# Storing one row of the first tile early, on ScalarE's queue, in an RMSNorm kernel

## The chip, the cores and the metric

The kernel runs on one core of one Trainium2 chip. The metric is the device time of one execution in microseconds (us). A span in a profile is a little shorter than that time (161.6 us against 163.42 us for the same execution of the kernel before), because it begins at the first and ends at the last profiled event. Times are compared between runs of the same chip and session, as medians. Engine names: ACT is ScalarE, DVE is VectorE, SP is the engine whose queue issues most transfers here.

## The reference, cut to what matters

```python
x: (16, 1024, 512) float32; gamma: (512,) float32
rms = np.sqrt(np.mean(x ** 2, axis=-1, keepdims=True) + 1e-5)
out = (x / rms * gamma).astype(np.float32)
```

There are 16,384 rows of 2 KB. 33.55 MB are read and 33.55 MB are written, and there is little arithmetic per byte.

## The kernel before

The rows form four tiles. A tile is 128 partitions x 32 rows of 512 numbers: 64 KB per partition, 8 MB in all, contiguous per partition both in HBM and in SBUF. The kernel keeps three tiles in SBUF ("slots"), so tile 3 goes into slot 0 again, once tile 0 has been stored. All large transfers are issued on SP's queue, in program order.

```python
def load(t, slot, r0, r1):
    nc.sync.dma_start(out=slots[slot][:, r0:r1], in_=xv[t][:, r0:r1])
def store(t, slot, r0, r1):
    nc.sync.dma_start(out=ov[t][:, r0:r1], in_=slots[slot][:, r0:r1])

load(0, 0, 0, 16)
load(0, 0, 16, 32)
load(1, 1, 0, 32)
load(2, 2, 0, 32)
# ... gamma is broadcast to all partitions ...
def compute(slot, r0, r1):
    for g in range(r0, r1, G):      # G = 8 rows
        # ACT: 8 x Square with a sum per row, then one Sqrt
        # DVE: one reciprocal, then 8 x (row * rstd * gamma), in place
        # ...

compute(0, 0, 32)
store(0, 0, 0, 32)
compute(1, 0, 16)
store(1, 1, 0, 16)
load(3, 0, 0, 16)                   # waits until slot 0 is stored
load(3, 0, 16, 32)
compute(1, 16, 32)
store(1, 1, 16, 32)
compute(2, 0, 32)
store(2, 2, 0, 32)
compute(0, 0, 16)                   # tile 3
store(3, 0, 0, 16)
compute(0, 16, 32)
store(3, 0, 16, 32)
```

Of the kernel before, what the change touches and what calls it, by code (L numbers as in the profile page):

```python
# [1 line left out]

# [4 lines left out]


@with_exitstack
def kernel(  # L10
    ctx: ExitStack,
    tc: tile.TileContext,
    x: bass.AP,
    gamma: bass.AP,
    out: bass.AP,
):
    nc = tc.nc
    P = nc.NUM_PARTITIONS
    eps = 1e-5
    fp32 = mybir.dt.float32  # L20
    AF = mybir.ActivationFunctionType
    OP = mybir.AluOpType

    xf = x.flatten_outer_dims()
    of = out.flatten_outer_dims()
    N, D = xf.shape
    R = 32
    G = 8
    assert N == 4 * P * R

    xv = xf.rearrange("(t p r) d -> t p r d", p=P, r=R)
    ov = of.rearrange("(t p r) d -> t p r d", p=P, r=R)

    const = ctx.enter_context(tc.tile_pool(name="const", bufs=1))
    stats = ctx.enter_context(tc.tile_pool(name="stats", bufs=4))
    psum = ctx.enter_context(tc.tile_pool(name="psum", bufs=1, space=bass.MemoryType.PSUM))

    slots = [const.tile([P, R, D], fp32, name=f"slot{i}") for i in range(3)]
# [12 lines that stand above are left out]
    gamma_row = const.tile([1, D], fp32)  # L51
    nc.scalar.dma_start(out=gamma_row, in_=gamma.unsqueeze(0))
    ones_col = const.tile([1, P], fp32)
    nc.vector.memset(ones_col, 1.0)  # L54
    gamma_psum = psum.tile([P, D], fp32)
    nc.tensor.matmul(gamma_psum, ones_col, gamma_row, start=True, stop=True)  # L56
    gamma_b = const.tile([P, D], fp32)
    nc.vector.tensor_copy(out=gamma_b, in_=gamma_psum)  # L58

    eps_t = const.tile([P, 1], fp32)  # L60
    nc.vector.memset(eps_t, eps)  # L61
    sq_scratch = const.tile([P, D], fp32)

    def compute(slot, r0, r1):
        for g in range(r0, r1, G):
            ss = stats.tile([P, G], fp32, name="ss")
            rms = stats.tile([P, G], fp32, name="rms")
            rstd = stats.tile([P, G], fp32, name="rstd")
            for r in range(G):
                nc.scalar.activation(  # L70
                    out=sq_scratch,
                    in_=slots[slot][:, g + r, :],
                    func=AF.Square,
                    accum_out=ss[:, r : r + 1],
                )
            nc.scalar.activation(out=rms, in_=ss, func=AF.Sqrt, bias=eps_t, scale=1.0 / D)  # L76
            nc.vector.reciprocal(out=rstd, in_=rms)  # L77
            for r in range(G):
                nc.vector.scalar_tensor_tensor(  # L79
                    out=slots[slot][:, g + r, :],  # L80
                    in0=slots[slot][:, g + r, :],
                    scalar=rstd[:, r : r + 1],
                    in1=gamma_b,
                    op0=OP.mult,
                    op1=OP.mult,
                )

    compute(0, 0, 32)
    store(0, 0, 0, 32)
    compute(1, 0, 16)  # L90
    store(1, 1, 0, 16)
    load(3, 0, 0, 16)
# [5 lines that stand above are left out]
    compute(0, 0, 16)  # L98
# [5 lines that stand above are left out]
# [1 line left out]
_INS = ['x', 'gamma']  # L105
_OUTS = [((16, 1024, 512), 'float32')]


# [23 lines left out]
```

## Time and profile before

| | kernel before |
|---|---|
| time, three runs | 163.3 us median (163.19 to 163.88) |
| span of the profiled run | 161.6 us |
| ACT busy, DVE busy | 98.5 us (61%), 90.4 us (56%) |
| moved by DMA | 67.14 MB, 415 GB/s over the span |

These are lines of the page of the kernel before: the busy time of each engine, the share of the 16 DMA engines that was busy in each of 40 equal slices (in tenths), the DMA packets, and the queue of SP (q1).

```profile
span 161.6 us, 509 instructions
PE 2.0 (1%) x2; PEld 0.5 (0%) x2; DVE 90.4 (56%) x147; ACT 98.5 (61%) x274; POOL 0.2 (0%) x4
...
DMA  7999999989989999699699999999999799699991
...
DMA packets 1733, 67.14 MB, mean 415 GB/s; under 512 B 193, under 2 KB 193, under 8 KB 194
...
q1 hardware_dynamic: 1728, 67.11, 97.3%
```

ACT and DVE are idle for more than a third of the span. The DMA engines are busy throughout (the digits below 9 come from counting, as explained below). What counts is therefore how long each packet keeps its DMA engine. The packet records of the trace give that (they are read from the trace itself; no view of the profile prints them): a packet of 64 KB (one partition's part of a tile) takes 2.418 us, one of 32 KB takes 1.213 us, and on each engine one follows the other with no gap of note (the eight packets of tile 1 per engine took 19.37 us on the median engine, 2.421 us each). No 64 KB packet of this trace is shorter than 2.418 us. 16 engines x 65,536 B / 2.418 us is 434 GB/s, which is called line rate below.

The windows view makes packets visible that take longer. Here are four windows of the kernel before. The last two columns are the busy share of the DMA engines and the GB/s that they moved. Whole packets are counted at their start, so both can exceed what is possible (1.19 and 516 in the second line), but they do so together.

```profile
core 0: us, PE busy (x) PEld busy (x) DVE busy (x) ACT busy (x) POOL busy (x), PEclk, DMA share, GB/s
26.00:36.00 10.00, 0.00 (x0) 0.00 (x0) 8.72 (x16) 9.59 (x29) 0.00 (x0) 1.00 0.97 420
36.00:44.00 8.00, 0.00 (x0) 0.00 (x0) 7.36 (x12) 4.66 (x14) 0.00 (x0) 1.00 1.19 516
44.00:56.00 12.00, 0.00 (x0) 0.00 (x0) 7.46 (x14) 11.52 (x33) 0.00 (x0) 1.00 1.00 432
56.00:68.00 12.00, 0.00 (x0) 0.00 (x0) 10.72 (x18) 11.50 (x35) 0.00 (x0) 1.00 0.94 360
```

At line rate, 420 GB/s needs a share of 420 / 434 = 0.97, which is what the first line has. In the last window 360 GB/s need 0.83, but the share is 0.94: (0.94 - 360/433.6) x 12 us = 1.32 us per engine went by without bytes. This number is called the **stall** below. (From the rounding of the share it is good to about 0.06 us.) The packets show where it is: all 16 engines lengthen exactly one packet, the last load packet of tile 2, just before the first big store, from 2.418 to between 3.3 and 3.97 us.

The chain of waits of the kernel before shows what hangs on it (start, length, what):

```profile
44.85 37.78 DMA out_dram<-slot
82.64 19.40 DMA slot<-in_x_dram
```

The store of tile 0 is issued at 44.85 us, but on its queue it stands behind the load of tile 2, which lands at 63.30 us, and it has landed only at 82.6 us. Tile 3 is loaded then.

### The profile page before, as it was taken

To read this page: it belongs to the slowest core of one execution; us is meant where nothing else is said; L and a number is where in the kernel's file an instruction comes from. 1 tells how busy PE (TensorE), PEld (TensorE's weight loads), DVE (VectorE), ACT (ScalarE), POOL (GpSimd) and SP (SyncE) were. 2 spreads that over 40 slices of the span, in tenths; PEclk is the share of its full clock that TensorE was granted. 3 is DMA by queue.
4 is the path that set the end of the run, shared out by engine and by line. 5 is a ranking of instruction groups with operands and counts; after the bars stand their busy time and mean duration, and the time that the engine had idled before them with its cause. 6 is when DMAs were issued, how large, how long until landed. Compare 5 with 4: busy or idle time off the path is not lost.

```text
span 161.6 us, 509 instructions
## 1 busy us (share of the span) xinstructions
PE 2.0 (1%) x2; PEld 0.5 (0%) x2; DVE 90.4 (56%) x147; ACT 98.5 (61%) x274; POOL 0.2 (0%) x4
## 2 busy tenths in 40 slices
PE   4000000000000000000000000000000000000000
PEld 1000000000000000000000000000000000000000
DVE  0100098988909898898898892019889880000000
ACT  3007999996599999999999700799999400000000
POOL 0000000000000000000000000000000000000000
DMA  7999999989989999699699999999999799699991
GB/s 260 389 430 478 389 470 438 519 375 405 519 373 405 505 276 487 292 519 487 292 440 454 389 454 454 389 478 430 389 503 519 308 487 503 292 462 430 405 470 49
DMA packets 1733, 67.14 MB, mean 415 GB/s; under 512 B 193, under 2 KB 193, under 8 KB 194
## 3 DMA queue, kind: packets, MB, share of 16 engines
q1 hardware_dynamic: 1728, 67.11, 97.3%
q14 instruction: 3, 0.02, 0.0%
q10 hardware_dynamic: 2, 0.00, 0.0%
HBM read 33.56 MB, written 33.55 MB: 415 GB/s over the span
## 4 chain that ended last, share of the span: by engine, by line
DMA 43%; ACT 20%; DVE 17%; issue 2%; DVEq 0%
DMA out_dram<-slot 23%; DMA slot<-in_x_dram 19%; ACT sq_scratch L70 18%; DVE slot L79 16%; ACT rms L76 2%; ACT L76 1%; DVE rstd L77 1%; DVEq L127 0%
## 5 line engine op out<-in xcount | busy, mean ns | idle before, releaser
L70 ACT ACTIVATE sq_scratch<-slot 128x512 f32<-128x512 f32 x128 | 80.5, 629 | 26.8 <-DMA slot<-in_x_dram 23.2
L79 DVE SCALAR_TENSOR_TENSOR slot<-slot,rstd,gamma_b 128x512 f32<-128x512 f32 x128 | 86.2, 747 | 0.6
L77 DVE RECIPROCAL rstd<-rms 128x8 f32<-128x8 f32 x16 | 3.2, 203 | 37.7 <-ACT rms L76 37.7
L70 ACT ACTIVATION_READ_ACCUMULATOR sq_scratch<-slot 128x1 f32 x128 | 23.9, 187 | 0.0
L76 ACT ACTIVATE rms<-ss,eps_t 128x8 f32<-128x8 f32 x16 | 4.8, 301 | 0.5
L58 DVE COPY gamma_b<-gamma_psum 128x512 f32<-128x512 f32 x1 | 0.7, 692 | 3.3 <-PE gamma_psum L56 3.3
L56 PE MATMUL gamma_psum<-gamma_row,ones_col 1*128 1x512 f32 x2 | 2.0, 1119 | 2.2 <-DMA gamma_row<-in_gamma_dram 2.2
L70 ACT ACT_TABLE_LOAD x1 | 1.3, 1283 | 1.3 <-PEq L116 1.3
L76 ACT ACT_TABLE_LOAD x1 | 1.3, 1283 | 0.0
L54 DVE MEMSET ones_col<- 1x128 f32 x1 | 0.2, 165 | 0.8 <-PEq L116 0.8
L56 PEld LDWEIGHTS gamma_psum<-gamma_row,ones_col 1*128 1x128 f32 x2 | 0.5, 308 | 2.2 <-issue 2.2
L116 POOL MEMSET const-bfloat16-1.0<- 128x1 bf16 x1 | 0.1, 101 | 0.0
L116 POOL MEMSET const-uint8-127<- 128x1 uint8 x1 | 0.1, 101 | 0.0
L116 POOL MEMSET const-float32-0.0<- 128x1 f32 x1 | 0.1, 98 | 0.2 <-issue 0.2
L116 POOL MEMSET const-float32-1.0<- 128x1 f32 x1 | 0.1, 98 | 0.0
L61 DVE MEMSET eps_t<- 128x1 f32 x1 | 0.1, 59 | 0.0
## 6 DMA issues: line engine op xcount, KB each, us to landing
slot<-in_x_dram SPq DMA_DIRECT2D x4, 4096.0 KB, 19.4
out_dram<-slot SPq DMA_DIRECT2D x4, 4096.0 KB, 31.2
slot<-in_x_dram SPq DMA_DIRECT2D x2, 50.9
out_dram<-slot SPq DMA_DIRECT2D x2, 40.5
gamma_row<-in_gamma_dram ACTq DMA_DIRECT2D x1, 2.0 KB
```

The lines of the kernel that those rows point to most:

```text
L54: nc.vector.memset(ones_col, 1.0)
L56: nc.tensor.matmul(gamma_psum, ones_col, gamma_row, start=True, stop=True)
L58: nc.vector.tensor_copy(out=gamma_b, in_=gamma_psum)
L61: nc.vector.memset(eps_t, eps)
L70: nc.scalar.activation(out=sq_scratch, in_=slots[slot][:, g + r, :], func=AF.Square, accum_out=ss[:, r : r + 1],)
L76: nc.scalar.activation(out=rms, in_=ss, func=AF.Sqrt, bias=eps_t, scale=1.0 / D)
L77: nc.vector.reciprocal(out=rstd, in_=rms)
L79: nc.vector.scalar_tensor_tensor(out=slots[slot][:, g + r, :], in0=slots[slot][:, g + r, :], scalar=rstd[:, r : r + 1], in1=gamma_b, op0=O ...
L116: nc = _bacc.Bacc("TRN2", target_bir_lowering=False, num_devices=1)
```

## The change: its intent, and the diff

The intent is to begin storing earlier: one finished row of each partition (256 KB in all) leaves on ACT's queue while the loads on SP's queue still run. The bytes are the same, and only their order changes.

```diff
-    compute(0, 0, 32)
-    store(0, 0, 0, 32)
+    compute(0, 0, G)
+    nc.scalar.dma_start(out=ov[0][:, 0:1], in_=slots[0][:, 0:1])
+    compute(0, G, 32)
+    store(0, 0, 1, 32)
```

## The prediction

> **What bounds the kernel now.** The DMA engines. The page gives ACT 61% and DVE 56% of the 161.6 us span, but its DMA row is filled to the end: 67.14 MB at a mean of 415 GB/s. In the windows view a share of 1.21 goes with 524 GB/s, so 16 fully busy engines move about 433 GB/s[...]. At that rate 67.1 MB need 155 us. About 6.6 us are left: about 2 us before the first packet, about 1.3 us after the last, stragglers, and packets slower than line rate.
>
> The trace's DMA packets show those. A 64 KB packet takes 2.418 us and a 32 KB one 1.213 us nearly everywhere, back to back. Two exceptions: the first load packet of each engine (about +0.56 us), and the last load packet in front of the first store, at about 58 to 62 us, where every engine took 3.3 to 3.97 us (about +1.3 us, once). The windows view agrees: 56 to 60 us has share 1.00 with only 295 GB/s, which needs 0.68. No later store start costs over about 0.1 us. I read it as a one-time cost of the core's first store to HBM; that is not proved.
>
> **What the change does.** Bytes stay the same. 256 KB (128 packets of 2 KB, eight per DMA engine) leave the first big store, whose packets shrink from 64 to 62 KB, and go out from ACT's queue. The instruction order puts that issue on ACT after the second Square of the second group, at about 21.9 us; DVE has row 0 ready at about 21.5 us. The issue costs ACT 0.34 to 0.53 us (DMA issues in the trace), and ACT idles 3.15 us before slot 1's first Square at 42.3 us: free. The big store is issued at about 45 us either way, and its turn comes only at about 62 us: free. The small store shares the same 16 engines with the loads[...], delays them by about 0.6 us and shortens the first store by as much. If the engines switch queues after each packet, I estimate eight rounds of about 2.5 us: landing at about 42 us, far before load 3 needs slot 0 at about 82 us.
>
> Cost: a 2 KB packet took 0.116 us (gamma's), line rate is 0.076 us: about 0.3 us for eight, perhaps more for turning between loads and stores.
> Gain: if the first-store cost is paid by the small store while loads keep the engine moving, up to 1.3 us disappears. If it blocks the engine there too, it only moves to about 22 us.
> All of this is on the critical path, since every DMA microsecond is.
>
> I weigh the two about equally: gain 0.65 us, cost 0.3 us.
>
> **Prediction: 162.9 us, range 161.8 to 164.3; faster by over 2% 0.02, within 2% 0.96, slower by over 2% 0.02.**
>
> **What would show it.** Right: unchanged ACT and DVE busy times; 56 to 62 us at about 433 GB/s per full share; load 2 landing at about 62 us instead of 63.3, and the first store about 1 us before 82.6. Gain wrong: the excess appears at about 22 us and later landings don't move. Cost wrong: share without bytes between 22 and 42 us above 0.3 us.
>
> **What would make it wrong.** Small packets stalling the loads at every switch (slower by 1 us or more); 62 KB packets off line rate; the slowest engine, about 1 us behind the others now, delayed further.

## The result, and the profile after

| | before | after |
|---|---|---|
| time, six fast runs each | 163.38 us median (163.03 to 163.88) | 163.2 us median (162.72 to 163.64) |
| ratio | | 0.9986, 95% interval 0.9962 to 1.0011: the same |
| span of the profiled run | 161.6 us | 161.1 us |

A ratio is the mean time of one kernel's fast runs over that of the other's of the same rounds, so it is not quite the ratio of the medians. No difference can be told from the scatter.

The page of the changed kernel, same lines as above, and with them the row of the issued transfers that is new (size in KB, us from issue to landing):

```profile
span 161.1 us, 510 instructions
PE 2.0 (1%) x2; PEld 0.5 (0%) x2; DVE 90.4 (56%) x147; ACT 98.6 (61%) x274; POOL 0.2 (0%) x4
...
DMA  7999999969999896999799999999999799699992
...
DMA packets 1877, 67.14 MB, mean 417 GB/s; under 512 B 209, under 2 KB 209, under 8 KB 338
...
q1 hardware_dynamic: 1728, 66.85, 97.1%
q10 hardware_dynamic: 146, 0.26, 0.4%
...
out_dram<-slot ACTq DMA_DIRECT2D x1, 256.0 KB, 23.8
```

And its timeline around the issue (start, length, what):

```profile
20.74 2.08 DVE L79 SCALAR_TENSOR_TENSOR slot<-slot,rstd,gamma_b 128x512 f32<-128x512 f32 x3
...
21.11 0.63 ACT L70 ACTIVATE sq_scratch<-slot 128x512 f32<-128x512 f32 x1
21.52 0.39 ACTq L89 DMA_DIRECT2D out_dram<-slot  x1
...
21.96 0.63 ACT L70 ACTIVATE sq_scratch<-slot 128x512 f32<-128x512 f32 x1
```

The small store is issued at 21.52 us, costs ACT under 0.2 us (the next Square starts at 21.96 us, and at 21.86 us in the kernel before), and lands 23.8 us later. In the packet records each of its 2 KB packets takes 0.084 us, and most of them have a 64 KB load packet on either side: they run in rounds of 16, which begin at 26.45, 28.95, 31.44, 33.94, 36.43, 38.92 and 41.42 us, with the eighth right behind the seventh at 41.77 us. So here the two queues took turns on one set of 16 engines. The windows and the chain of the changed kernel:

```profile
26.00:36.00 10.00, 0.00 (x0) 0.00 (x0) 8.63 (x16) 9.59 (x29) 0.00 (x0) 1.00 1.00 433
36.00:44.00 8.00, 0.00 (x0) 0.00 (x0) 7.36 (x13) 4.24 (x12) 0.00 (x0) 1.00 0.95 410
44.00:56.00 12.00, 0.00 (x0) 0.00 (x0) 7.01 (x13) 11.53 (x34) 0.00 (x0) 1.00 1.01 438
56.00:68.00 12.00, 0.00 (x0) 0.00 (x0) 10.76 (x18) 11.49 (x34) 0.00 (x0) 1.00 1.07 423
```

```profile
44.94 37.45 DMA out_dram<-slot
82.46 19.45 DMA slot<-in_x_dram
```

The stall is still there: (1.07 - 423/433.6) x 12 us = 1.13 us, against 1.32 us before. And nothing was lengthened at 26 to 44 us, where the small store ran: 0.05 us in all. So the core had already written to HBM when the big store began, and the engines waited all the same. My reading of the stall was wrong, and the experiments look for what it is.

### The profile page after: what moved, and what is told of

It reads as the page before. It is cut to its first block, busy times and chain, and to the rows that moved or that the text cites. A ratio compares the mean times of both kernels' runs of the same rounds, so it can differ in the third digit from the quotient of the medians.

```text
span 161.1 us, 510 instructions
## 1 busy us (share of the span) xinstructions
PE 2.0 (1%) x2; PEld 0.5 (0%) x2; DVE 90.4 (56%) x147; ACT 98.6 (61%) x274; POOL 0.2 (0%) x4
## 4 chain that ended last, share of the span: by engine, by line
DMA 43%; ACT 20%; DVE 17%; issue 2%; DVEq 0%; ACTq 0%; SPq 0%
DMA out_dram<-slot 23%; DMA slot<-in_x_dram 20%; ACT sq_scratch L70 18%; DVE slot L79 16%; ACT rms L76 2%; ACT L76 1%; DVE rstd L77 1%; DVEq L129 0%; ACTq L89 0%; SPq L41 0%
## 6 DMA issues: line engine op xcount, KB each, us to landing
out_dram<-slot ACTq DMA_DIRECT2D x1, 256.0 KB, 23.8
```

## The experiments

The theories at the start, for the stall at 56 to 62 us:

- *issue*: it is a collision with the next store's issue at 60.5 us;
- *ring*: the first store on SP's own queue pays it;
- *size*: any 64 KB load packet followed by a store packet pays it;
- *bulk*: the first store of some length pays it, and 2 KB packets are too short.

Later ones split *bulk* into a *write side* (HBM is written for the first time, either anywhere or in each region) and a *read side* (DMA reads SBUF for the first time: until then there had been loads only, which write SBUF). In the expectations, S is the stall. The runs e, f and g were made on three chips, and a time is compared only with the kernel before on the same chip.

### Four first looks

**e1_slot1_whole**: nothing is issued at 60.5 us.

```diff
-    compute(1, 0, 16)
-    store(1, 1, 0, 16)
+    compute(1, 0, 32)
+    store(1, 1, 0, 32)
     load(3, 0, 0, 16)
     load(3, 0, 16, 32)
-    compute(1, 16, 32)
-    store(1, 1, 16, 32)
```

> Edit to the kernel before: slot 1 is stored by one 8 MB DMA after its whole compute, so that no DMA is issued near 60.5 us, where before issued the store of slot 1's first half. Stall S is the lengthening of the last load packet of each engine before the first big store (about 1.3 us per engine before, 1.14 after). Theory issue (S is a collision with the DMA issue at 60.5 us): S falls below 0.3 us and load 2 lands about 1 us earlier than 63.3. Theories ring (first store on the SP queue pays), bulk (first large store pays) and size (64 KB load packet followed by a store packet pays): S stays at 1.0 to 1.4 us.

Measured: the stall is 1.34 us, load 2 lands at 63.53 us; 163.65 us (before 163.25). *Issue* falls.

**e2_small_on_sp**: the small store of the change, on SP's queue between loads 1 and 2.

```diff
-    load(2, 2, 0, 32)      # with the other loads
     compute(0, 0, G)
-    nc.scalar.dma_start(out=ov[0][:, 0:1], in_=slots[0][:, 0:1])
+    store(0, 0, 0, 1)
+    load(2, 2, 0, 32)
```

> Edit to the changed kernel: the same 256 KB store, but issued on SP's queue between load 1 and load 2, so it runs at about 41 us as the first store of that queue. Theory ring: S at about 58 to 62 us falls below 0.3 us, and about 1 us of lengthening shows at about 39 to 43 us instead. Theory bulk: nothing over 0.3 us at 41 us, S stays 1.0 to 1.4 us at 62. Theory size: about 1 us at 41 us and again at 62 us. Theory issue: S stays at 62.

Measured: 0.38 us at 36 to 44 us, and 0.65 us at 56 to 68 us; 163.11 us (before 163.25). No theory had this. The eight 2 KB packets ran one after the other here, and on ACT's queue they ran mostly one at a time between load packets. One after the other they paid a part, and the big store paid the rest.

**e3_eight_rows**: the early store takes all eight finished rows, on ACT's queue.

```diff
-    nc.scalar.dma_start(out=ov[0][:, 0:1], in_=slots[0][:, 0:1])
+    nc.scalar.dma_start(out=ov[0][:, 0:8], in_=slots[0][:, 0:8])
     compute(0, G, 32)
-    store(0, 0, 1, 32)
+    store(0, 0, 8, 32)
```

> Edit to the changed kernel: all eight finished rows (16 KB per partition, 2 MB) go out early on ACT's queue, not one. Theory bulk: 0.5 us or more of lengthening of load packets right at the first 16 KB packets, at about 27 to 30 us, and S at 62 us below 0.5 us. Theories ring, size and issue: S stays at 1.0 to 1.4 us at about 62 us, and the early packets run within 0.05 us of line rate.

Measured: no stall at the big store (0.01 us), but 0.55 us at 26 to 36 us and 0.47 us at 36 to 44 us; 162.38 us (before 163.25). *Bulk* holds and *ring* falls, since the big store was still the first store on SP's queue. The packets show two steps: the load packet in front of the first 16 KB packet is lengthened by about 0.4 us, and the last load packet of tile 1, at about 42 us, by about 0.4 us again.

**e4_halves**: the kernel before, with 32 KB packets on both sides of the first load-to-store switch.

```diff
-    load(2, 2, 0, 32)
+    load(2, 2, 0, 16)
+    load(2, 2, 16, 32)
 ...
-    store(0, 0, 0, 32)
+    store(0, 0, 0, 16)
+    store(0, 0, 16, 32)
```

> Edit to the kernel before: load 2 and store 0 in two halves each, so the last load packet and the first store packet are 32 KB, as at the later load-to-store switch at 110 us, which cost 0.1 us. Theory size: S falls to 0.1 to 0.6 us. Theories ring, bulk and issue: S stays at 1.0 to 1.4 us.

Measured: 1.31 us; 163.97 us (before 163.25). *Size* falls.

### Which side of the store pays

All edits are to the changed kernel. In the expectations of f1 and f4 the theory *core* is a write side that is paid once, wherever HBM is written. In f1, f3 and f4 tile 0 is stored whole at its usual turn, and the 2 MB of the early transfer come on top: an estimate of 2.10 MB / 434 GB/s = 4.8 us.

**f1_other_address** (rows written to the wrong place, and overwritten later):

```diff
-    nc.scalar.dma_start(out=ov[0][:, 0:1], in_=slots[0][:, 0:1])
+    nc.scalar.dma_start(out=ov[3][:, 0:8], in_=slots[0][:, 0:8])
```

> Edit to the eight-row run: the early 2 MB go to the place of the last tile's output (they are overwritten later by the right rows), and the whole of tile 0 is stored at its usual turn. Adds 2 MB, about 4.8 us at 433 GB/s. Theory core (what is paid is a warm-up of the write path of each engine, wherever it writes): S at the first big store (now about 67 us) below 0.3 us, as in the eight-row run. Theory address (each engine pays for the output region that it first writes): S there is 0.8 us or more.

Measured: 0.65 us at 26 to 36 us, 0.23 us at 36 to 44 us, and 0.00 us at the big store; 167.17 us (before 163.03). Where in the output the early store wrote made no difference at the big store (0.00 us here, 0.01 us in e3). *Address* falls.

**f2_few_partitions**: the bytes of the change as one 16 KB packet per engine.

```diff
-    nc.scalar.dma_start(out=ov[0][:, 0:1], in_=slots[0][:, 0:1])
+    nc.scalar.dma_start(out=ov[0][0:16, 0:8], in_=slots[0][0:16, 0:8])
 ...
-    store(0, 0, 1, 32)
+    nc.sync.dma_start(out=ov[0][16:128], in_=slots[0][16:128])
+    nc.sync.dma_start(out=ov[0][0:16, 8:32], in_=slots[0][0:16, 8:32])
```

> Edit to the changed kernel: the same 256 KB go early, but as eight rows of 16 partitions: one 16 KB packet per engine in place of eight of 2 KB. Theory packet (what matters is the length of one unbroken write, and 2 KB is too short to pay anything): about 0.4 us at the early packet, at about 29 to 32 us, and S at 62 us clearly below the 1.14 us of the changed kernel, at 0.9 us or less. Theory amount (bytes written before count, whatever their cut): S at 62 us 1.0 to 1.3 us, as in the changed kernel, which wrote the same bytes. Theory address: S 1.0 to 1.3 us too, since one packet covers only an eighth of the engine's rows.

Measured: 174.43 us (before 163.03), and inconclusive for the question, because the edit brought a larger effect of its own. Its windows have 0.61 us at 26 to 36 us and 1.01 us at 56 to 68 us, so the big store kept more than the 0.9 us that *packet* allowed, as *amount* expected. But in both windows other packets than the last loads were slow too (the early 16 KB ones by 0.55 us on average), so this is no clean count of the stall. Here is its window with the store of the 16 partitions' remaining rows:

```profile
80.00:92.00 12.00, 0.00 (x0) 0.00 (x0) 10.72 (x18) 11.49 (x34) 0.00 (x0) 1.00 0.94 203
```

The engines are busy and move 203 GB/s. Of that store's sixteen 48 KB packets, eleven took 6.9 us longer on average than the 1.81 us of line rate (8.8 us in all), and the engines stayed out of step to the end. The other five ran at line rate or close to it. What slowed the eleven was not shown: no run here tests a transfer of few partitions alone.

**f3_sbuf_to_sbuf**: SBUF is read early by DMA, but HBM is not written.

```diff
-    load(2, 2, 0, 32)      # with the other loads
+    load(2, 2, 0, 24)
 ...
-    nc.scalar.dma_start(out=ov[0][:, 0:1], in_=slots[0][:, 0:1])
+    nc.scalar.dma_start(out=slots[2][:, 24:32], in_=slots[0][:, 0:8])
+    load(2, 2, 24, 32)     # loads over the copied rows
```

> Edit to the eight-row run: the early 2 MB go from slot 0 to rows 24 to 32 of slot 2 (loaded over afterwards by a load of its own), so SBUF is read early by DMA but HBM isn't written; tile 0 is stored whole at its turn. Adds 2 MB, about 4.8 us. Theory read side (S is the first read of SBUF by DMA): about 0.4 us at the first early packet, and S at the first big store below 0.3 us. Theory write side (S is the first bulk write to HBM): no stretch at the early packets, S 1.0 to 1.4 us.

**f4_hbm_to_hbm**: HBM is written early by DMA, but SBUF is not read.

```diff
-    nc.scalar.dma_start(out=ov[0][:, 0:1], in_=slots[0][:, 0:1])
+    nc.scalar.dma_start(out=ov[3][:, 0:8], in_=xv[3][:, 0:8])
```

> Edit to the eight-row run: the early 2 MB go from the input's last tile straight to the output's last tile (overwritten later), issued by ACT at the start, so HBM is written early by DMA but SBUF isn't read; tile 0 is stored whole at its turn. Adds 2 MB, about 4.8 us. Theory write side with core: S at the first big store below 0.3 us. Theory read side: S 1.0 to 1.4 us. Theory address: S 0.8 us or more.

The windows of f3_sbuf_to_sbuf:

```profile
26.00:36.00 10.00, 0.00 (x0) 0.00 (x0) 8.41 (x15) 9.31 (x28) 0.00 (x0) 1.00 1.14 473
36.00:44.00 8.00, 0.00 (x0) 0.00 (x0) 7.36 (x13) 3.25 (x10) 0.00 (x0) 1.00 0.83 328
...
56.00:68.00 12.00, 0.00 (x0) 0.00 (x0) 10.72 (x18) 11.53 (x33) 0.00 (x0) 1.00 1.05 451
```

and those of f4_hbm_to_hbm:

```profile
26.00:36.00 10.00, 0.00 (x0) 0.00 (x0) 9.32 (x15) 9.59 (x28) 0.00 (x0) 1.00 0.97 419
36.00:44.00 8.00, 0.00 (x0) 0.00 (x0) 6.75 (x12) 6.49 (x20) 0.00 (x0) 1.00 1.20 517
...
56.00:68.00 12.00, 0.00 (x0) 0.00 (x0) 10.72 (x18) 11.50 (x35) 0.00 (x0) 1.00 0.91 350
```

With the copy inside SBUF the early windows have 0.49 and 0.59 us without bytes, and the window of the first big store has 0.12 us, none of it at the switch: tile 2's last load packets (16 KB) and the first store packets run at line rate, 0.611 and 2.418 us. With the copy inside HBM the early windows have 0.04 and 0.06 us, and the big store pays 1.23 us. The times agree: 167.24 us and 168.65 us (before 163.03), which less 4.8 us are about 162.4 and 163.8 us. So **in these runs the stall belongs to the first long read of SBUF by DMA, and not to the first write to HBM.** One reservation: the copy of f4 ran from the start and had landed at 20.1 us, over 40 us before the big store's turn, while the copy of f3 landed at 53.1 us. The copy of f4 shows no bill of its own, though: in the first 20 us, by the packet records, its engines spent only 0.15 us more above line rate than those of the kernel before. And f3 by itself shows that no HBM write is needed to pay the bill. What in the read takes the time, no run shows.

### Is the bill smaller when it is paid early?

**g2_eight_rows_on_sp**: the 2 MB of the eight-row store, unbroken, on SP's queue.

```diff
-    load(2, 2, 0, 32)      # with the other loads
     compute(0, 0, G)
-    nc.scalar.dma_start(out=ov[0][:, 0:1], in_=slots[0][:, 0:1])
+    store(0, 0, 0, 8)
+    load(2, 2, 0, 32)
     compute(0, G, 32)
-    store(0, 0, 1, 32)
+    store(0, 0, 8, 32)
```

> The eight-row store on SP's queue between load 1 and load 2: the same 2 MB, now as an unbroken run of eight 16 KB packets per engine, not between load packets. Theory first bulk read of SBUF pays, whatever queue issues it: 0.9 to 1.3 us of lengthening at about 39 to 43 us, S before the big store below 0.2 us, and no gain in time over the changed kernel beyond its scatter. Rival (only the mixing with loads, or ACT's queue, removes S): S before the big store stays 0.6 us or more.

Its windows:

```profile
36.00:44.00 8.00, 0.00 (x0) 0.00 (x0) 7.36 (x13) 3.99 (x12) 0.00 (x0) 1.00 0.98 367
...
56.00:68.00 12.00, 0.00 (x0) 0.00 (x0) 10.91 (x17) 11.49 (x34) 0.00 (x0) 1.00 0.96 415
```

Measured: 1.07 us at 36 to 44 us and 0.04 us at the big store; 163.71 us, with 163.67 us before. The bill moved, all of it, and no time was won.

**g3_four_rows** (edit as in e3 with 4 for 8: 8 KB packets):

> Four rows early on ACT's queue (8 KB packets, 1 MB), between the one row of the change (S 1.14 us) and eight rows (S 0). If the payment depends on the length of a packet in steps between 2 and 16 KB: early lengthening of 0.1 to 0.4 us per engine at the first early packet and S at 62 us between 0.1 and 0.8 us. If any packet of more than a few KB pays in full: S below 0.1 us.

Measured: 0.19, 0.40 and, at the big store, 0.32 us; 162.47 us (before 163.67).

**g4_sixteen_rows** (edit as in e3 with 16 for 8, and compute(0, 0, 16) ahead of it: 32 KB packets), five rounds:

> Sixteen rows early on ACT's queue (32 KB packets, 4 MB), issued at about 33 us; candidate for a version that beats both. If the gain of eight rows comes from S being paid in parts between loads: early lengthening 0.8 to 1.1 us in all, S before the big store below 0.1 us, and a time like eight rows, ratio 0.993 to 0.998. If longer packets pay the whole at once: 1.2 us or more early, ratio 0.997 to 1.001.

Measured: 1.24 us in one step at 32 to 36 us, 0.00 us at the big store. 162.83 us median (162.5 to 163.09, six runs) against 163.67 us; ratio 0.9945, 95% interval 0.9929 to 0.9961.

**g1_eight_rows_timed**: the kernel of e3 again, five rounds.

> The eight-row kernel again, unchanged, timed against the kernel before. Its one look was 0.87 us shorter than before's. If its gain is the vanished S and a less delayed slowest engine: 0.4 to 1.1 us faster, ratio 0.993 to 0.998 with an interval below 1, and S at 62 to 67 us again below 0.1 us. If the one look was luck: ratio 0.998 to 1.002.

Measured: 162.47 us median (162.39 to 162.68, six runs) against 163.67 us (163.37 to 164.15, eleven runs); ratio 0.9927, 95% interval 0.9911 to 0.9943. This is the best version: 0.7% faster than the kernel before, clear of the scatter, though well under 2%. The changed kernel was not timed in the same session. Its own ratio to the kernel before was 0.9986, and the two intervals don't overlap. The windows of this kernel:

```profile
26.00:36.00 10.00, 0.00 (x0) 0.00 (x0) 8.52 (x16) 9.39 (x29) 0.00 (x0) 1.00 1.12 460
36.00:44.00 8.00, 0.00 (x0) 0.00 (x0) 7.36 (x13) 3.12 (x9) 0.00 (x0) 1.00 0.86 344
44.00:56.00 12.00, 0.00 (x0) 0.00 (x0) 4.50 (x9) 9.59 (x27) 0.00 (x0) 1.00 1.01 437
56.00:68.00 12.00, 0.00 (x0) 0.00 (x0) 10.72 (x19) 11.52 (x33) 0.00 (x0) 1.00 0.96 416
```

### The bill, and where 0.7% came from

All the runs but f2 side by side, computed as above; the last column is how far the last DMA engine finished behind the median engine in the last store, from the 16 completions of that store in the trace.

| run | early transfer: queue, packet | 26-36 | 36-44 | 44-56 | 56-68 us | sum | last engine behind |
|---|---|---|---|---|---|---|---|
| before | none | 0.01 | 0.00 | 0.05 | 1.32 | 1.38 | 1.58 |
| after | ACT, 2 KB | 0.01 | 0.04 | 0.00 | 1.13 | 1.18 | 1.27 |
| e1 | none | 0.01 | 0.00 | 0.05 | 1.34 | 1.40 | 1.85 |
| e2 | SP, 2 KB | 0.01 | 0.38 | 0.00 | 0.65 | 1.04 | 1.87 |
| e4 | none | 0.01 | 0.01 | 0.08 | 1.31 | 1.41 | 2.22 |
| g3 | ACT, 8 KB | 0.19 | 0.40 | -0.01 | 0.32 | 0.90 | 1.13 |
| e3 | ACT, 16 KB | 0.55 | 0.47 | 0.03 | 0.01 | 1.06 | 0.98 |
| g1 (same kernel) | ACT, 16 KB | 0.59 | 0.53 | 0.03 | 0.01 | 1.16 | 0.94 |
| f1 | ACT, 16 KB | 0.65 | 0.23 | 0.03 | 0.00 | 0.91 | 1.05 |
| f3 | ACT, 16 KB, SBUF to SBUF | 0.49 | 0.59 | 0.05 | 0.12 | 1.25 | 1.01 |
| f4 | ACT, 16 KB, HBM to HBM | 0.04 | 0.06 | 0.03 | 1.23 | 1.36 | 2.11 |
| g2 | SP, 16 KB | 0.01 | 1.07 | 0.13 | 0.04 | 1.25 | 2.09 |
| g4 | ACT, 32 KB | 1.24 | 0.01 | 0.03 | 0.00 | 1.28 | 1.17 |

The sum stays between 0.9 and 1.4 us in every run of the table: an early read of SBUF moved the bill and took about a third off it at most (1.38 to 0.90 us). In these runs, how much of it moved grew with the stretch that was read without a load packet in between. With 2 KB packets that ran mostly one by one (after) it hardly moved (1.13 us were left at the big store); with 16 KB packets between loads it moved altogether (0.01 us left in e3), and with 32 KB ones in a single step (1.24 us in g4). In g3, e3 and g4 the packets and the amount grew together, but the amount alone doesn't decide: e2 and the changed kernel read the same bytes early in the same 2 KB packets, and where eight ran in one row the big store was left with 0.65 us, otherwise with 1.13 us (the queue and the moment differed too). The second step of e3 fits: after it two 16 KB packets ran in a row, on 15 of the 16 engines. A run that holds the amount fixed and changes only the packet is missing, since f2 failed at it.

That does not yet explain why g1 (162.47 us) is faster than g2 (163.71 us, one run), which stores the same eight rows. The last column does. In these two profiled runs the median engine finished the last store at 159.05 us before and at 158.72 us in g1 (0.33 us earlier), and the last engine 1.58 us behind it before and 0.94 us in g1 (0.64 us less). Two thirds of the 0.97 us thus come from the one engine that ends last. Its lag grows in the kernel before from 1.08 us at the landing of load 3's first half to 1.56 us at that of its second half, at 112.3 us, where the queue turns from loads to stores again. In g1 it stays at 0.97 us there, and in g2 it jumps from 1.29 to 2.08 us. In all six runs with an early read of SBUF on ACT's queue in packets of 8 KB or more (e3, f1, f3, g1, g3, g4) the lag grows there by 0.11 us or less, and in the changed kernel by 0.12 us (1.12 to 1.24 us). In the others (before, e1, e2, e4, f4, g2) it grows by 0.28 us or more. That is a regularity over single profiles. Part of the lag may have a visible origin. In every page that was taken (before, after, f2, f3, f4, g1, g2) the DMA queues include q14, of kind "instruction", with three packets in the span. In the kernel before these are 8 KB each and run at 33.97, 53.25 and 82.87 us between the other packets: 0.31 us each on the engine that they hit, with the following packet lengthened by 0.31, 0.60 and 0.12 us. Followed from end to start, the packets of g1 show that the engine hit by the one at 56.8 us (0.31 us, and 0.53 us on the next packet, 0.84 us in all) is the one that ended last, with a lag of 0.94 us; in the kernel before, the same holds for the one at 53.3 us as far as the packets can be told apart. No run tests it. Why a read on ACT's queue long before spares the last engine this second delay is open.

## Why the prediction was right or wrong

- **The bound (DMA engines at line rate, about 434 GB/s): right.** ACT and DVE stayed at 98.6 and 90.4 us busy, as predicted, and the time didn't move beyond the scatter. But the changes that the prediction named as its test did not come: load 2 landed at 63.66 us (before 63.30 us, expected about 62 us), and the first store 0.23 us earlier (82.39 us) instead of about 1 us.
- **"DVE has row 0 ready at about 21.5 us", issue on ACT at about 21.9 us, free: right.** It was issued at 21.52 us and took 0.39 us; ACT's waiting for loads is 23.0 us where it was 23.2 us.
- **Landing at about 42 us: the turns were right and the time 3 us short.** It landed at 45.3 us (21.52 + 23.8). The first 2 KB packet ran only at 26.5 us, some 5 us after the issue. It harmed nothing: tile 3's load was issued at 82.46 us.
- **Cost 0.3 us for eight small packets: too high.** They took 0.084 us each where 2 KB at line rate need 0.076 us: 8 x 0.008 = 0.06 us per engine. 62 KB packets ran at line rate (2.342 us).
- **Gain 0.65 us, the mean of "disappears" and "only moves to about 22 us": this is the step that failed.** It rested on the sentence "I read it as a one-time cost of the core's first store to HBM". Neither of its two outcomes came. The small store paid nothing, and the stall stayed where it was, at 1.13 us of 1.32 us, because in these runs it is paid by the first long read of SBUF (f3 left 0.12 us at the big store, f4 1.23 us), and 2 KB packets that ran one by one between loads hardly paid it. In place of 0.65 us the stall shrank by 0.19 us, or by 0.15 us if the 16 lengthened packets themselves are averaged (from 1.28 to 1.14 us).
- **The sum held by luck, because both terms were too large.** Predicted: 0.65 - 0.3 = 0.35 us net, 162.9 us. The terms as measured, 0.19 - 0.06 (or 0.15 - 0.06), make about 0.1 us; the median engine gained 0.13 us in the last store (159.05 to 158.92 us). The time is 163.2 us, inside the range, but the range of 161.8 to 164.3 us also held the time before, 163.38 us, so it could not tell a right mechanism from a wrong one. Of the alternatives I had named, "it only moves" was the one to believe, for a store long enough to pay: g2 showed it (1.07 us at 36 to 44 us, 0.04 us at the big store).

## What to carry to other kernels

Where the DMA engines are the bound, look at single packets: bytes per busy share in a window find time that no engine's idle row shows (here 360 GB/s at a share of 0.94). The one-time cost found so here was not, or only in part, saved by paying it earlier on the same saturated engines (1.38 us in sum before, 0.90 us at the lowest); ask first whether anything is idle when it falls due. And before explaining a stall in front of a store by the store's write, separate its two ends with a copy inside SBUF and a copy inside HBM, since the write may be innocent (here the first left 0.12 us at the big store, the second 1.23 us).
